# Starts of small tables and of the tiles behind them moved to multiples of 128 bytes, in a four-layer model on one core

## The chip, the cores and the metric

The program runs on one core of a Trainium2 chip. The metric is the device time of one execution in microseconds. Three runs of the kernel before gave 2496.11, 2497.12 and 2497.93 us; the median is 2497.12 us.

## What is computed

Two blocks of two layers each work on 256 tokens of width 1024 in float32. In the first block a layer is a mixer (projections of the normed input, a gated recurrence by chunks and three dilated attentions, two branches, an output projection) and a feed-forward with a squared ReLU. In the second block a layer is another mixer, then a dense SwiGLU (layer 0) or eight experts of which each token takes two (layer 1), then a gate. Cut to the large products:

```python
def first_block(...):
    for l in range(2):
        z = rms_norm(x, norm1_g[l]) @ w_in[l]                     # 1024 x 8704
        y = sigmoid(za) * (o_hg @ w_branch_a[l]) + sigmoid(zb) * (o_att @ w_branch_b[l])
        x = x + y @ w_out[l]
        x = x + square(relu(rms_norm(x, norm2_g[l]) @ w_up[l])) @ w_down[l]   # 4096 wide

def second_block(...):
    for i in range(2):
        h = h + hybrid_mixer(rmsnorm(h, norm_mix[i]), w_in[i], ..., w_out[i], i)
        xn = rmsnorm(h, norm_ffn[i])
        h = h + (swiglu(xn, ...) if i == 0 else moe_swiglu(xn, router, wg, wu, wd))
        h = h + sigmoid(rmsnorm(h, ple_norm[i]) @ ple_gate[i]) * (p[i] @ ple_proj[i])

def moe_swiglu(xn, router, wg, wu, wd):        # eight experts, 1024 x 3584 each, top two
    for e in range(8):
        out = out + combine[:, e:e+1] * ((silu(t @ wg[e]) * (t @ wu[e])) @ wd[e])
```

## The kernel before, in words

**The products.** Every weight matrix is cut into tiles of up to 512 rows by 512 columns, in the order of use (class `Plan`). `Kernel.ahead` fetches a tile by a DMA on SyncE's queue into a buffer `raw`, ScalarE rounds it to `hi` (line 435), VectorE takes the rest `lo = raw - hi` (line 436). An activation is turned by TensorE (`tr`, line 484) and split in the same way into a hi and a lo part (`tsplit`, lines 492 and 493; with a gain: `gained`, lines 501 and 503). `mm3` then makes each product of three matmuls, lines 450, 451 and 452: hi by hi, lo by hi, hi by lo. In each the activation's part, 128 by 128, is loaded into the array (here: the loaded operand), and the weight's part, 512 columns, streams past it. Each of the three loads its own 128 by 128, so every matmul has a load ahead of it.

**Where the loaded operands live.** `n` are the normed activations (pool `na`, whole program). `l` are split activations of the stage at hand (pool `lg`): in the first block they feed branches, output projection and down projection, in the second the projection of `p`, the output projection and the dense down projection, in the experts the down projections. The last expert's down operands are in a pool of their own, `lx`, named `x` in the profile. `o` is the 0/1 matrix that scatters an expert's rows back (lines 1508 and 1509). Operands of short matmuls are in `t`, `h` and others.

**What sets the addresses.** Tiles take addresses in the order in which their pools are opened, one behind the other, each rounded up to 32 bytes per partition. `const` and the weight buffers come first, then `sm` (small statistics, 64 bytes each, line 310), then `na`. For each stage `Kernel.open` lays a new scope behind that: `sc` (single tiles), `lg`, `tmp` and others. The second block first opens `ppp` and `sec` for good; `sec` holds the tables `tri`, `half` (2 columns, 8 bytes) and `iota`, which `fetch` (line 613) allocates, and the router's weights. In the experts, `route` (line 1389) first allocates `comb`, `rank`, `sel`, `count`, `most`, `rst`, then `unit` and the rows; the pools of the experts come behind them. Twelve bytes of `rst` or eight of `half` thus shift everything behind them in their scope.

**The order.** TensorE's order is the program's; the other engines are ordered by a scheduler. The change leaves the order of every engine as it was.

Of the kernel before, what the change touches and what calls it, by code (L numbers as in the profile page):

```python
# [10 lines left out]
BF16 = mybir.dt.bfloat16  # L11
U8 = mybir.dt.uint8
I32 = mybir.dt.int32
# [66 lines left out]
class Plan:  # L80


    def __init__(self):
        self.tiles = []
        self.specs = {}
        self.where = {}
        self.size = {}
        for l in range(2):
            self.first(l)
        self.mix2(0, lambda: self.rows("pp", 0))  # L90
        self.dense()
        self.gate2(0)
        self.mix2(1, lambda: self.rows("pp", 1))
        self.moe()
# [205 lines left out]
class Kernel:  # L300
    def __init__(self, tc, io, ctx):
        self.tc = tc
        self.nc = tc.nc
        self.io = io
        pool = lambda name, bufs, **k: ctx.enter_context(tc.tile_pool(name=name, bufs=bufs, **k))
        self.const = pool("const", 1)
        self.raw_p = pool("raw", RAW)
        self.hi_p = pool("hi", NSPLIT)
        self.lo_p = pool("lo", NSPLIT)
        self.sm = pool("sm", 40)  # L310
        self.na = pool("na", 8)
        self.acc_p = pool("acc", 4, space=PSUM)
        self.ms_p = pool("ms", 4, space=PSUM)
        self.scope = None
        self.plan = Plan()
        self.specs = self.plan.specs
        self.n_dma = self.n_split = self.n_used = 0
        self.rawt = {}
        self.split = {}
        self.flip = 0  # L320
        self.urgent = []
        self.tasks = []
        self.now = 0
        self.rate = 2
        self.grain = GRAIN1
        self.fetching = 0
        self.ring = deque([self.raw_p] * RAW)
        self.queue = None
# [284 lines left out]
    def fetch(self, name, dt=F32, pool=None):  # L613
        nc, src = self.nc, self.io["c_" + name]
        queue = self.queue or nc.gpsimd
        n = src.shape[1]
        t = (pool or self.sc).tile([128, n], dt, name=name)
        self.fetching += 1

        def gen():  # L620
            yield 3
            if dt == F32:
                queue.dma_start(t, src)
            else:
                for c in range(0, n, 384):
                    m = min(384, n - c)
                    r = self.T((128, m))
                    queue.dma_start(r, src[:, c:c + m])
                    nc.gpsimd.tensor_copy(t[:, c:c + m], r)
                    yield 1  # L630
            self.fetching -= 1
        self.push(gen())
        return t
# [755 lines left out]
    def route(self, norm, ms):  # L1389
        nc = self.nc  # L1390
        small = lambda name, shape, dt=F32: self.sc.tile([128, *shape], dt, name=name)
        self.comb, self.rank, self.sel = small("comb", (2, 8)), small("rank", (2, 8)), small("sel", (2, 8))
        self.count, self.most = small("count", (8,), I32), small("most", (1,), I32)
        self.rst = small("rst", (3, 2), BF16)
        self.unit = small("unit", (128,), BF16)
        nc.vector.tensor_copy(self.unit, self.ident)
        self.rows = [[[small(f"x{n}{b}{h}", (512,), BF16) for n in range(3)] for h in range(2)] for b in range(2)]
        self.need(lambda: ms[2] == 4)
        for h in range(2):
            for b in range(2):  # L1400
                self.thirds(self.xs(b, h), self.rows[b][h], self.T())
        self.spin(SPIN)
        with self.soon(HPR):
            top, s0, s1 = self.pick(ms[:2])

        def rest():
            yield 2
            cnt = self.M(8)
            for b in range(2):
                nc.tensor.matmul(cnt, self.ones, self.sel[:, b], start=b == 0, stop=b == 1)  # L1410
            self.thirds(norm.rst, [self.rst[:, n] for n in range(3)], self.S(2))
            e, g = self.S(2, 2), self.S(2, 2)
            R = norm.ready()
            for b in range(2):
                nc.vector.tensor_scalar(e[:, b, 0:1], top[:, b, 1:2], top[:, b, 0:1], R[b], op0=ALU.subtract, op1=ALU.mult)
            nc.scalar.activation(e[:, :, 1], e[:, :, 0], AF.Exp)
            nc.vector.tensor_scalar(e[:, :, 0], e[:, :, 1], 1.0, None, op0=ALU.add)
            nc.vector.reciprocal(g[:, :, 0], e[:, :, 0])
            nc.vector.tensor_mul(g[:, :, 1], g[:, :, 0], e[:, :, 1])
            for b in range(2):  # L1420
                nc.vector.tensor_scalar(s0[:, b], s0[:, b], g[:, b, 0:1], None, op0=ALU.mult)
                nc.vector.scalar_tensor_tensor(self.comb[:, b], s1[:, b], g[:, b, 1:2], s0[:, b], op0=ALU.mult, op1=ALU.add)
            most = self.S(1)
            nc.vector.tensor_reduce(most, cnt, axis=AX.X, op=ALU.max)
            nc.vector.tensor_copy(self.count, cnt)
            nc.vector.tensor_copy(self.most, most)
        self.push(rest())
# [398 lines left out]
```

## Time and profile before

| | us |
|---|---|
| median of three runs | 2497.12 |
| the profiled execution's own time | 2501.25 |
| its span, first to last instruction | 2499.4 |
| TensorE matmul busy | 2464.4 |
| VectorE busy | 1922.3 |
| ScalarE busy | 1618.6 |
| mean granted TensorE clock | 0.992 |

The profiled execution took 4.1 us longer than the median of the runs, and 1.9 us of its time lie outside the span. Busy times of TensorE are modelled: the record of one matmul reaches over the start of the next, so it is the distance from start to start, in the timeline, that says how fast matmuls follow one another. The first block runs from 0 to about 950 us, the second block without the experts to about 1470 us (its dense feed-forward from about 1100 to 1275 us), the experts from there to about 2460 us.

### The profile page before, as it was taken

How to read it: one execution, taken by the hardware profiler on the slowest of the kernel's cores; microseconds unless marked ns; L12 is line 12 of the kernel's file. 1: busy time of each engine (PE TensorE's matmuls, PEld its weight loads, DVE VectorE, ACT ScalarE, POOL GpSimd, SP SyncE). 2: the span in 40 equal slices, each digit the busy share in tenths (PEclk: the TensorE clock that was granted, in tenths of full speed). 3: DMA queues.
4: the chain of work that ended last, by engine and by line, in shares of the span. 5: the costliest groups of instructions: out<-in, count | busy, mean ns of one | idle time of the engine just before them, and what ended most of it. 6: DMA issues, size and time to landing. Idle time of an engine off the chain costs nothing. (4 is left out here: it accounts for less than half of the span.)

```text
span 2499.4 us, 33937 instructions
## 1 busy us (share of the span) xinstructions
PE 2464.4 (99%) x12113; PEld 2040.2 (82%) x12113; DVE 1922.3 (77%) x3330; ACT 1618.6 (65%) x2667; POOL 47.5 (2%) x66
## 2 busy tenths in 40 slices
PE   9999999999999999999999999999999999999998
PEld 7888888888888887888888878888888888888786
DVE  7775765578667656775576879999898989898888
ACT  7555555575556546654557567777777777777675
POOL 1000000100000002000001000000000000000000
PEclk9999999999999999999999989999999999999999
DMA  7443555553345555344564469999899999977895
GB/s 277 158 146 125 179 178 188 198 201 144 135 152 191 175 176 200 106 169 169 199 214 162 166 273 354 356 354 361 342 348 357 353 356 349 361 285 290 322 342 194
DMA packets 90530, 600.16 MB, mean 240 GB/s; under 512 B 12576, under 2 KB 14368, under 8 KB 19568
## 3 DMA queue, kind: packets, MB, share of 16 engines
q1 hardware_dynamic: 84240, 591.27, 64.2%
q10 hardware_dynamic: 4928, 3.16, 0.5%
q0 software_dynamic: 1184, 3.48, 0.4%
q8 instruction: 97, 1.59, 0.2%
q14 instruction: 81, 0.66, 0.1%
HBM read 596.82 MB, written 1.05 MB: 239 GB/s over the span
## 5 line engine op out<-in xcount | busy, mean ns | idle before, releaser
L436 DVE TENSOR_TENSOR lo<-raw,hi 128x512 fp32r<-128x512 f32 (+3 forms) x1584 | 1384.2, 911 | 315.9 <-ACT hi L435 296.7
L435 ACT CAST hi<-raw 128x512 fp32r<-128x512 f32 (+3 forms) x1584 | 1198.2, 800 | 422.6 <-PE a L451 340.1
L450 PE MATMUL a<-hi,n 128*128 128x512 f32 (+2 forms) x2176 | 867.9, 399 | 4.6 <-PEq L1661 3.5
L452 PE MATMUL a<-lo,n 128*128 128x512 f32 (+2 forms) x2176 | 848.9, 390 | 0.0
L451 PE MATMUL a<-hi,n 128*128 128x512 f32 (+2 forms) x2176 | 845.7, 389 | 1.7 <-DVE n L503 1.7
L452 PEld LDWEIGHTS a<-lo,n 128*128 128x128 f32 x2176 | 410.4, 189 | 93.3 <-DVE lo L436 5.1
L451 PEld LDWEIGHTS a<-hi,n 128*128 128x128 f32 x2176 | 411.7, 189 | 81.5 <-DVE n L503 3.2
L450 PEld LDWEIGHTS a<-hi,n 128*128 128x128 f32 x2176 | 411.1, 189 | 81.8 <-issue 4.2
L450 PE MATMUL a<-hi,l 128*128 128x512 f32 x552 | 220.3, 399 | 0.0
L452 PE MATMUL a<-lo,l 128*128 128x512 f32 x552 | 216.2, 392 | 0.0
L451 PE MATMUL a<-hi,l 128*128 128x512 f32 x552 | 216.1, 391 | 0.0
L492 ACT CAST l<-m 128x512 fp32r<-128x512 f32 (+1 forms) x126 | 70.2, 559 | 150.8 <-PE m L484 150.8
L450 PE MATMUL m<-hi,l 128*128 128x512 f32 x400 | 158.9, 397 | 0.7 <-ACT l L492 0.7
L451 PE MATMUL m<-hi,l 128*128 128x512 f32 x400 | 158.3, 396 | 0.2 <-DVE l L493 0.2
L452 PE MATMUL m<-lo,l 128*128 128x512 f32 x400 | 158.1, 395 | 0.0
L493 DVE TENSOR_TENSOR l<-m,l 128x512 fp32r<-128x512 f32 (+1 forms) x126 | 82.5, 658 | 62.4 <-ACT l L492 62.3
L452 PEld LDWEIGHTS a<-lo,l 128*128 128x128 f32 x552 | 103.7, 188 | 23.2
L451 PEld LDWEIGHTS a<-hi,l 128*128 128x128 f32 x552 | 103.8, 188 | 21.1
L450 PEld LDWEIGHTS a<-hi,l 128*128 128x128 f32 x552 | 103.7, 188 | 21.0
L484 PE MATMUL m<-ident,t 128*128 128x128 f32 x652 | 99.0, 272 | 2.8 <-DVE t L567 2.1
L484 PEld LDWEIGHTS m<-ident,t 128*128 128x128 f32 x652 | 80.3, 140 | 22.4 <-DVE t L567 2.6
L450 PEld LDWEIGHTS m<-hi,l 128*128 128x128 f32 x400 | 75.2, 188 | 18.4 <-ACT l L492 0.9
(302 smaller groups left out, 1784.7 us busy)
## 6 DMA issues: line engine op xcount, KB each, us to landing
raw<-in_w_dram SPq DMA_DIRECT2D x553, 1024.0 KB, 5.1
raw<-in_w_dram SPq DMA_DIRECT2D x10, 512.0 KB, 3.4
raw<-in_w_dram SPq DMA_DIRECT2D x4, 520.0 KB, 4.1
t<-in_c_dil_dram POOLq DMA_DIRECT2D x6, 192.0 KB, 2.9
x<-in_x_dram SPq DMA_DIRECT2D x4, 256.0 KB, 7.1
raw<-in_w_dram SPq DMA_DIRECT2D x4, 256.0 KB, 6.8
dec<-in_c_dec_dram POOLq DMA_DIRECT2D x2, 512.0 KB, 7.8
out_dram<-x SPq DMA_DIRECT2D x4, 256.0 KB, 2.0
```

What stands on the lines that cost most here:

```text
L435: nc.scalar.copy(hi[:, p], t[:, q])
L436: nc.vector.tensor_sub(lo[:, p], t[:, q], hi[:, p].bitcast(F32))
L450: mm(out, ah, wh, start=start, stop=False)
L451: mm(out, al, wh, start=False, stop=False)
L452: mm(out, ah, wl, start=False, stop=stop)
L484: self.nc.tensor.transpose(p[:, j], src[:, j * 128:(j + 1) * 128], self.ident)
L492: nc.scalar.copy(hi, p[:, :m])
L493: nc.vector.tensor_sub(lo, p[:, :m], hi.bitcast(F32))
```

## The change

The pool `sm` shrinks from 40 tiles to 38, that is by 128 bytes. `half` is allocated as 128 bytes, of which 8 are used. In `route`, `most` becomes 32 bytes, `rst` 32 bytes, and a tile `rest` of 96 bytes is allocated that nothing uses.

```diff
-        self.sm = pool("sm", 40)
+        self.sm = pool("sm", 38)
...
-        t = (pool or self.sc).tile([128, n], dt, name=name)
+        t = (pool or self.sc).tile([128, max(n, 32)], dt, name=name)[:, :n]
...
-        self.count, self.most = small("count", (8,), I32), small("most", (1,), I32)
-        self.rst = small("rst", (3, 2), BF16)
+        self.count, self.most = small("count", (8,), I32), small("most", (8,), I32)[:, 0:1]
+        self.rst = small("rst", (8, 2), BF16)[:, 0:3]
+        small("rest", (24,))
```

No instruction is added, removed or moved. What moves is the start of the tiles. In the built programs the loaded operands of matmuls with 512 streamed columns start at these places, in bytes past a multiple of 256 (the 128 loaded columns are 512 bytes wide, so all slices of a tile share its place):

```
loaded operand, and where               matmuls   before   after
n, all projections from a norm             6336        0     128
l, first block                             1152        0     128
l, second block before the experts          504       32       0
l, experts                                 1200       64     128
x, last expert                              144       64     128
o, scatter                                   64       64     128
streamed hi and lo, everywhere                -        0       0
```

In the second block and the experts the tiles `t`, the rows (bfloat16) and the tables move in the same way, from 32 or 64 bytes past a multiple of 128 to a multiple of 128. The `raw` buffers at the far end of the memory stay where they were.

With 38 tiles in the ring of `sm` a tile comes round two allocations sooner, so one wait for GpSimd stands earlier. On VectorE, in the attention of the second block's mixer (line 1086 finds a row's maximum, lines 1221 and 1222 mix two softmaxes; `Pool_49` is GpSimd's semaphore), as a piece of the difference:

```order
 L1221 TENSOR_SCALAR t<-t,s 128x256
 L1088 TENSOR_SCALAR s<-s 128x1 [waits DVE_49]
-L1086 ISA t,s<-m,caus 128x256 [waits PE_49]
+L1086 ISA t,s<-m,caus 128x256 [waits PE_49,Pool_49]
 L1086 ISA s 128x1
 L1222 SCALAR_TENSOR_TENSOR t<-t,s 128x256 [waits DVE_49]
 L1088 TENSOR_SCALAR s<-s 128x1 [waits DVE_49]
-L1086 ISA t,s<-m,caus 128x128 [waits PE_49,Pool_49]
+L1086 ISA t,s<-m,caus 128x128 [waits PE_49]
```

The wait moved four rows up, from one maximum to the one before it; the same happens once in the second mixer, and once on ScalarE.

## Rows read from the trace of the kernel before

**Rows 1.** The page, part 1: busy us (share of the span) and instructions.
```profile
span 2499.4 us, 33937 instructions
PE 2464.4 (99%) x12113; PEld 2040.2 (82%) x12113; DVE 1922.3 (77%) x3330; ACT 1618.6 (65%) x2667; POOL 47.5 (2%) x66
```
**Rows 2.** Windows: us, busy PE, PEld, DVE, ACT, POOL, clock, DMA share, GB/s.
```profile
1200.00:1300.00 100.00, 100.00 (x498) 83.51 (x497) 63.10 (x136) 55.20 (x123) 2.06 (x4) 1.00 0.58 203
...
1500.00:1600.00 100.00, 100.00 (x487) 81.74 (x486) 93.14 (x92) 79.96 (x89) 0.00 (x0) 1.00 0.94 359
```
**Rows 3.** Waits, SyncE 1500:2000, ScalarE and TensorE 2000:2400: us in total, times, longest.
```profile
SPq L418 <- DVE lo L436: 420.9, 164, 6.1
...
ACT hi L435 <- DMA raw<-in_w_dram: 1.0, 2, 0.6
...
PE a L450 <- PEq L1661: 3.5, 1, 3.5
```
**Rows 4.** Timeline of PE, first block, down projection, operand at 0: start us, busy us.
```profile
456.00 0.39 PE L450 MATMUL a<-hi,l 128*128 128x512 f32 x1
...
458.72 0.39 PE L450 MATMUL a<-hi,l 128*128 128x512 f32 x1
```
**Rows 5.** Timeline of PE, first block, branch projection, operand at a multiple of 256.
```profile
261.34 0.39 PE L452 MATMUL a<-lo,l 128*128 128x512 f32 x1
...
263.15 0.39 PE L451 MATMUL a<-hi,l 128*128 128x512 f32 x1
```
**Rows 6.** Timeline of PE, second block, dense down projection, operand at 32.
```profile
1250.43 0.40 PE L450 MATMUL a<-hi,l 128*128 128x512 f32 x1
...
1253.23 0.40 PE L450 MATMUL a<-hi,l 128*128 128x512 f32 x1
```
**Rows 7.** Timeline of PE, experts: down projection (l at 64), then up (n at 0).
```profile
1610.26 0.39 PE L452 MATMUL m<-lo,l 128*128 128x512 f32 x1
...
1613.06 0.39 PE L452 MATMUL m<-lo,l 128*128 128x512 f32 x1
...
1616.08 0.39 PE L450 MATMUL a<-hi,n 128*128 128x512 f32 x1
...
1617.67 0.39 PE L451 MATMUL a<-hi,n 128*128 128x512 f32 x1
```
**Rows 8.** Timeline of PE, first block, just behind short matmuls, operand at 0.
```profile
150.92 0.39 PE L451 MATMUL a<-hi,n 128*128 128x512 f32 x1
...
153.00 0.39 PE L451 MATMUL a<-hi,n 128*128 128x512 f32 x1
```
**Rows 9.** Groups by form, line 452, a third of each product's matmuls.
```profile
L452 PE MATMUL a<-lo,n 128*128 128x512 f32 x2112 | 830.8, 393 | 0.0
...
L452 PE MATMUL a<-lo,l 128*128 128x512 f32 x552 | 216.2, 392 | 0.0
...
L452 PE MATMUL m<-lo,l 128*128 128x512 f32 x400 | 158.1, 395 | 0.0
...
L452 PE MATMUL m<-lo,x 128*128 128x512 f32 x48 | 19.2, 399 | 0.3 <-DVE lo L436 0.3
```
**Rows 10.** Line 492, first block, then experts: duration ns min/median/max, first and last start.
```profile
L492 ACT CAST l<-m x48: 573/578/587, 128.9 to 859.5; 128x512 fp32r<-128x512 f32 x48
...
L492 ACT CAST l<-m x47: 573/585/587, 1512.1 to 2326.0; 128x512 fp32r<-128x512 f32 x47
```
**Rows 11.** Timelines of POOL and DVE, mixer of the second block's layer 1.
```profile
1328.27 0.60 POOL L1247 TENSOR_SCALAR l<-tri,s 128x128 f32<-128x128 f32 x1
...
1337.95 0.28 DVE L1086 CUSTOM_DVE_ANT_0 t<-m,caus 128x128 f32<-128x128 f32 x1
```
**Rows 12.** Timeline of PE, dense up projection, 256 columns, operand at 0.
```profile
1203.61 0.28 PE L452 MATMUL a<-lo,n 128*128 128x256 f32 x1
...
1205.04 0.28 PE L452 MATMUL a<-lo,n 128*128 128x256 f32 x1
```

## The prediction

> **What bounds the kernel now.** I began with the busy times: TensorE is busy for 99% of the span, VectorE for 77% [rows 1]. A modelled busy time proves little, so the windows came next. In the dense down projection and all through the experts TensorE shows no idle time; in the experts VectorE is at 93 of 100 us and the DMAs at 0.94 of theirs, at 359 GB/s [rows 2]. Then the waits say who follows whom. From 2000 to 2400 us TensorE's longest wait is 3.5 us at the branch of the overflow path, ScalarE waits 1.0 us in all for weights to land, and SyncE's queue waits 420.9 us of 500 for VectorE to give a buffer back [rows 3]. So weights are ready early and fetches are held up by buffers: TensorE sets the pace, and a nanosecond taken off each of its matmuls should come off the end, so long as nothing else is that close.
>
> The decisive view is the timeline of TensorE, read from start to start. In long runs of equal matmuls, 512 columns each, the reader is to divide the distance of two starts by the matmuls between them:
>
> - loaded operand at a multiple of 512 bytes: 12 matmuls from 456.00 to 458.72, 226.7 ns each [rows 4];
> - at a multiple of 256: 8 from 261.34 to 263.15, 226.3 ns [rows 5];
> - 32 bytes past a multiple of 128, dense down projection: 12 from 1250.43 to 1253.23, 233.3 ns [rows 6];
> - 64 bytes past it, experts' down projection: 12 from 1610.26 to 1613.06, 233.3 ns; three microseconds later, in the same stage, the up projection with n at 0: 7 from 1616.08 to 1617.67, 227.1 ns [rows 7].
>
> [...] The streamed operand is at 0 everywhere, so it explains nothing.
>
> **The change part by part.**
>
> *Loaded operands at 32 or 64 bytes.* The groups give a third of the matmuls each [rows 9]: m<-lo,l 400 and m<-lo,x 48 are the experts' down projections, 3 x 448 = 1344 matmuls; of a<-lo,l's 552 the placement puts 384 at 0 and 168 at 32, so 3 x 168 = 504 matmuls of the second block. If the load then costs what it costs in rows 4, each gains 6.7 ns. That isn't quite so where short matmuls stand ahead: there nine matmuls with an operand at 0 take 2.08 us, 231.1 ns [rows 8], and the gain would be 2.2 ns. Bounds for the 1848: 12.3 us if all are in long runs, 4.1 us if none is. The experts' downs come in runs of 24 that follow other long matmuls, as around rows 7, so I take the full 6.7 ns: 9.0 us. In the second block's projections about a quarter stand behind transposes or attention (117 of 453 recorded, counted along the timeline): 504 x (0.75 x 6.7 + 0.25 x 2.2) = 2.8 us. Sum **11.8 us**.
>
> *Small ones.* The 64 scatter loads of `o` (0 to 0.4 us), and the first three matmuls behind each experts' down run, which take 0.69 us where 0.68 would do (1615.39 to 1616.08 by the same timeline; some 50 times, 0.5 us). The gathers' bfloat16 operands move too; no row has them at a multiple of 128, and I take 0, with 0 to 1 us for the range. Transposes of `t` at 32 and 64 show the same 272 ns as those at 0: nothing.
>
> *VectorE, ScalarE, DMAs.* Their tiles move as well. ScalarE's line 492 writes l at 0 in the first block and at 64 in the experts: medians 578 and 585 ns, minimum 573 in both [rows 10]. Nothing to gain there, and nothing on the path. The `raw` buffers don't move.
>
> *The ring of 38.* The earlier wait for GpSimd stands on VectorE's line 1086. GpSimd is done at 1328.87, the first such instruction starts at 1337.95 [rows 11]; in the mixer before and on ScalarE the distance is no smaller. It costs nothing; without those 9 us of lead, VectorE and the split of weights behind it would wait for GpSimd.
>
> *What goes the other way.* To free bytes, `sm` lost 128, and n and the first block's l moved from 0 to 128 past a multiple of 256. No row of this trace shows a matmul of 512 columns with its operand there. Cost 0 if 128 is as good as 256, and 6.7 ns for each of 7488 matmuls if it isn't (a rival below). [...]
>
> [...]
>
> The profiled execution would go from 2501.25 to 2489.5 us. It stands 4.1 us above the median of the runs, so the median goes from 2497.12 to 2485.3; I say **2485 us**.
>
> **The rivals.**
>
> *Blocks of 256 bytes (slower).* [...] It decides at n, whose start goes to 128 past 256. Price: (6336 + 1152) x 6.7 = 50 us more, less 504 x 6.7 = 3 us for the second block's l, which goes to 0; the experts' downs stay as slow as they are. That is 2497 + 47 = 2544 at most; with a third of the n matmuls behind short ones, where the loss is 2.2 ns, 2533. I take 2538.
>
> *The start is not the cause (no change).* The chains at 233 ns are all of later stages, so stage and start go together; then the time stays at 2497. Against it: within the experts, 3 us apart, n runs at 227 and l at 233 [rows 7], and the dense down projection has the form of the first block's [rows 4, 6].
>
> [...]
>
> *The DMAs become the bound of the experts.* TensorE would ask for 0.9% more than 359 GB/s at a share of 0.94 [rows 2]. For it: that is close. Against it: 1.0 us of waiting for weights [rows 3]. Then the 9.0 us are lost and 2.8 stay: 2494.3.
>
> **How the numbers follow.** A difference of 0.2%, 5 us, is about what a measurement of this kernel can tell from none. Forecast 0.78 (14.2 us, 2482.9, with long runs throughout and all small gains; 2493 at the lower bound of 4.1 us), slower by blocks of 256 0.12, no change 0.05, DMAs 0.05. Range 2482 (2482.9 less the 0.9 us by which runs scatter) to 2494.5: the forecast and the DMA case, 0.83. Faster 0.78; same 0.10, which is no change and the DMA case; slower 0.12.
>
> **What would show it.** Right: the runs that answer to rows 6 and 7 fall to 2.72 us for 12 matmuls, those of rows 4, 5 and 12 stay, the experts' stage ends some 12 us earlier. Wrong: n at 233 ns in the first block, so that the down projection of rows 4 comes microseconds late; or downs still at 233; or downs at 227 while TensorE waits for `lo` or ScalarE for `raw` in the experts.

## The result, and the profile after

The changed kernel takes 2522.39 us (median of 5 runs, 2518.39 to 2523.40) against 2497.12 us for the kernel before beside it (2495.80 to 2501.16): a ratio of 1.0091, 95% interval 1.0079 to 1.0102. (The ratios are those on record for all runs of a comparison, not quotients of two medians; that quotient is 1.0101 here.) It is slower by 25.3 us where 12 us less was forecast, and 28 us above the upper end of the range.

The profiled execution took 2522.39 us, its span is 2520.6 us. Its page, part 1 (busy us, share of the span, instructions), answers to [rows 1]:

```profile
PE 2486.7 (99%) x12113; PEld 2043.2 (81%) x12113; DVE 1922.6 (76%) x3330; ACT 1619.5 (64%) x2667; POOL 46.9 (2%) x66
```

The instructions are the same in number. TensorE's busy time grew by 22.3 us and the span by 21.2; VectorE and ScalarE are where they were, within 1 us. The window, columns as in [rows 2], shows no idle time of TensorE either, and its longest wait from 2000 to 2420 us is still the one at the branch of the overflow path, 3.9 us where [rows 3] have 3.5:

```profile
1500.00:1600.00 100.00, 100.00 (x483) 81.22 (x482) 92.03 (x91) 78.86 (x88) 0.00 (x0) 1.00 0.95 361
```

So TensorE still sets the pace, at the same granted clock of 1.00 in this stretch, and its matmuls follow one another more slowly. The timeline of TensorE says which. First block, down projection, l now 128 past a multiple of 256 (before: [rows 4]):

```profile
455.91 0.39 PE L450 MATMUL a<-hi,l 128*128 128x512 f32 x1
...
458.69 0.40 PE L450 MATMUL a<-hi,l 128*128 128x512 f32 x1
```

Twelve matmuls in 2.78 us, 231.7 ns each, where it was 226.7. Second block, l now at a multiple of 256 (before at 32: [rows 6]):

```profile
1265.13 0.39 PE L451 MATMUL a<-hi,l 128*128 128x512 f32 x1
...
1267.85 0.39 PE L451 MATMUL a<-hi,l 128*128 128x512 f32 x1
```

Twelve in 2.72 us, 226.7 ns instead of 233.3: the gain that was forecast for it. Experts, down projection (l from 64 to 128), then up (n from 0 to 128), as in [rows 7]:

```profile
1625.46 0.39 PE L450 MATMUL m<-hi,l 128*128 128x512 f32 x1
...
1628.25 0.40 PE L450 MATMUL m<-hi,l 128*128 128x512 f32 x1
...
1631.04 0.39 PE L450 MATMUL a<-hi,n 128*128 128x512 f32 x1
...
1633.13 0.40 PE L450 MATMUL a<-hi,n 128*128 128x512 f32 x1
```

The down projection stays slow, 2.79 us for twelve (232.5 ns, before 233.3); n now takes 232.2 ns, 9 in 2.09 us, where it took 227.1. Two of the stretches in the rows of before don't lose. Just behind short matmuls, as in [rows 8], nine matmuls still take 2.08 us; and with 256 columns, as in [rows 12], twelve still take 1.43 us:

```profile
152.26 0.39 PE L451 MATMUL a<-hi,n 128*128 128x512 f32 x1
...
154.34 0.39 PE L451 MATMUL a<-hi,n 128*128 128x512 f32 x1
...
1218.15 0.28 PE L451 MATMUL a<-hi,n 128*128 128x256 f32 x1
...
1219.58 0.28 PE L451 MATMUL a<-hi,n 128*128 128x256 f32 x1
```

To turn such stretches into a sum, all distances from start to start of 512-column matmuls that follow one another, up to 260 ns, were averaged along the timeline for each product, and the difference to before was multiplied by the product's number of matmuls:

```
                            before    after    matmuls    difference
n                           228.67   232.62      6336      +25.0 us
l, first block              227.45   232.49      1152       +5.8
l, second block             233.27   227.59       504       -2.9
l and x, experts            233.28   232.56      1344       -1.0
sum                                                        +26.9      (measured +25.3)
```

The means of l in the experts stand for x as well. n's mean before is above 226.7 because of the stretches behind short matmuls. The whole loss is thus in place: n and the first block's l pay 30.8 us, and the two gains are worth 3.9.

### The profile page after: what moved, and what is told of

The parts are those of the page before. It is cut to its first block, busy times and chain, and to the rows that moved or that the text cites. A ratio compares the mean times of both kernels' runs of the same rounds, so it can differ in the third digit from the quotient of the medians.

```text
span 2520.6 us, 33937 instructions
## 1 busy us (share of the span) xinstructions
PE 2486.7 (99%) x12113; PEld 2043.2 (81%) x12113; DVE 1922.6 (76%) x3330; ACT 1619.5 (64%) x2667; POOL 46.9 (2%) x66
```

## The experiments

Three theories could explain this. **Blocks of 256**: a loaded operand is slow wherever its own start isn't a multiple of 256. **Ring**: the shorter ring of `sm` holds VectorE up, and the starts only go with it. **Padding**: the larger tiles cost the time. The first comparison tests these; its kernel before took 2498.60 us (median).

**All wide tiles at multiples of 256.** A ring of 32, `half` of 256 bytes, and a longer `rest`:

```diff
-        self.sm = pool("sm", 38)
+        self.sm = pool("sm", 32)
...
-        t = (pool or self.sc).tile([128, max(n, 32)], dt, name=name)[:, :n]
+        t = (pool or self.sc).tile([128, max(n, 64)], dt, name=name)[:, :n]
...
-        small("rest", (24,))
+        small("rest", (56,))
```

> Ring of 32 sm buffers; half, the last tile of the small-table area and the route tables padded so that n and every wide tile start at a multiple of 256 bytes (in the experts 256 past a multiple of 512). Theory 'blocks of 256' (a loaded operand of 128 float32 columns is slow wherever its start is not a multiple of 256): n and the first block's l stay at 227 to 229 ns, the second block's l goes from 233.3 to 227.6 (504 x 5.7 = 2.9 us), the experts' down projections from 233.4 to 227.6 (1344 x 5.8 = 7.8 us): 2497.1 - 10.7 = 2486.4 us. Theory 'ring' (the shorter ring of sm makes VectorE wait for GpSimd, the starts are only a sign of it): a ring of 32 is shorter still than 38, so at least 2522 us. Theory 'padding' (the larger tiles of the second block or the experts cost the time): about 2522 us.

Measured: 2490.27 us, ratio 0.9959, interval 0.9945 to 0.9972. Its experts' down projection:

```profile
1606.50 0.39 PE L450 MATMUL m<-hi,l 128*128 128x512 f32 x1
...
1609.22 0.39 PE L450 MATMUL m<-hi,l 128*128 128x512 f32 x1
```

226.7 ns each. On its page TensorE's busy time is 2452.4 us, 12.0 less than in [rows 1], and the ring of 32 and the larger padding cost nothing that can be seen. Ring and padding fall.

**The change with a ring of 36.** Everything behind `sm` lies 128 bytes lower, the padding is the change's:

```diff
-        self.sm = pool("sm", 38)
+        self.sm = pool("sm", 36)
```

> The change with a ring of 36 instead of 38 sm buffers, so that everything behind it lies 128 bytes lower: n and the first block's l at multiples of 256 again, the experts' wide tiles at a multiple of 256 too, the second block's l 128 past one. Blocks of 256: n and first l as before, second l from 233.3 to 232.5 (504 x 0.8 = 0.4 us), experts' downs 1344 x 5.8 = 7.8 us: 2497.1 - 8.2 = 2488.9 us. Ring: 2522 us or more. Padding: about 2522 us, since the padding is that of the change.

Measured: 2490.59 us, ratio 0.9969 (0.9958 to 0.9980). The mean of n is 228.5 ns again, of the experts' l 226.8, of the second block's l 232.3. One number in the first line of the change decides between a gain and a loss.

**n alone moved.** In the kernel before:

```diff
-        self.sm = pool("sm", 40)
-        self.na = pool("na", 8)
+        self.sm = pool("sm", 36); pool("gap", 1).tile([128, 32], F32, name="gap")
+        self.na = pool("na", 8); pool("gap2", 1).tile([128, 32], F32, name="gap2")
```

> The kernel before with n alone moved: 4 sm buffers fewer, 128 unused bytes ahead of n's pool and 128 behind it, so that only n lies 128 past a multiple of 256 and all else where it was. Blocks of 256: 6336 matmuls with n from a mean of 228.7 to 232.6 ns, 24.9 us: 2522.0 us; l's intervals as before. If n's start costs nothing and the loss of the change lies in l or elsewhere: 2497 us.

Measured: 2520.81 us, ratio 1.0083 (1.0068 to 1.0099). The mean of n is 232.75 ns, all three l's are within 0.2 ns of before. n's start alone carries most of the loss.

**The streamed operands alone moved.** A control, and the test of a fourth theory, which the expectation calls relation. In the kernel before, a ring of 38 and 128 bytes ahead of the weight buffers, so that hi and lo start at 128 (and `raw` 128 bytes higher), and all else stays.

```diff
-        self.raw_p = pool("raw", RAW)
+        pool("gap", 1).tile([128, 32], F32, name="gap"); self.raw_p = pool("raw", RAW)
...
-        self.sm = pool("sm", 40)
+        self.sm = pool("sm", 38)
```

> The kernel before with a ring of 38 sm buffers and 128 unused bytes ahead of the raw, hi and lo pools: the streamed operands hi and lo lie 128 past a multiple of 256, n, l and everything behind them exactly where they were. Blocks of 256 by the loaded operand's own start: 2497.1 us, n at 228.7. Theory 'relation' (what counts is the distance of the loaded operand's start from the streamed one's, which the change made 128 for n): n and first l slow, 24.9 + 5.8 us: 2527.8 us. Ring: 2522 us, since the ring is the change's 38.

Measured: 2523.18 us, ratio 1.0093 (1.0078 to 1.0109): slow, with every loaded operand exactly where the fast kernel had it. First block's l at 0, then the experts' l at 64, in its timeline:

```profile
455.08 0.39 PE L450 MATMUL a<-hi,l 128*128 128x512 f32 x1
...
457.88 0.39 PE L450 MATMUL a<-hi,l 128*128 128x512 f32 x1
...
1611.25 0.39 PE L450 MATMUL m<-hi,l 128*128 128x512 f32 x1
...
1613.99 0.39 PE L450 MATMUL m<-hi,l 128*128 128x512 f32 x1
```

l at 0 goes from 226.7 to 233.3 ns, and l at 64, slow before, to 228.3 in this stretch (2.74 us for twelve). Blocks of 256 by the loaded operand's own start falls, and so does a theory in which each operand needs a good start of its own, since the experts' l got faster by making the other operand's start worse. What is left is **relation**: the distance from the streamed operand's start to the loaded one's, modulo 256. I still set it against that last theory, **both starts**, in the next comparison (kernel before: 2499.14 us).

**The change, with the streamed operands moved along.** Every loaded operand stays where the change puts it:

```diff
-        self.raw_p = pool("raw", RAW)
+        pool("gap", 1).tile([128, 32], F32, name="gap"); self.raw_p = pool("raw", RAW)
...
-        self.sm = pool("sm", 38)
+        self.sm = pool("sm", 36)
```

> The change with every start as the change has it (n, first block's l and the experts' l 128 past a multiple of 256, second block's l at one), and only the streamed operands moved: 2 sm buffers fewer and 128 unused bytes ahead of raw, hi and lo, so that hi and lo too lie 128 past a multiple of 256. Theory 'relation' (a matmul is fast when the loaded operand's start lies a multiple of 256 from the streamed one's, whatever either is): n, first l and experts' l fast again, the second block's l at a distance of 128 and slow: 2497.1 - 1344 x 5.8 ns - 504 x 0.8 ns = 2488.9 us. Theory 'both starts' (each operand has to start at a multiple of 256 by itself): the loaded starts are the change's and the streamed ones now off too: 2522 us or more.

Measured: 2487.88 us, ratio 0.9960 (0.9946 to 0.9974). Experts, down and then up, all of them with both operands 128 past a multiple of 256:

```profile
1603.15 0.39 PE L450 MATMUL m<-hi,l 128*128 128x512 f32 x1
...
1605.87 0.39 PE L450 MATMUL m<-hi,l 128*128 128x512 f32 x1
...
1608.59 0.39 PE L450 MATMUL a<-hi,n 128*128 128x512 f32 x1
...
1610.63 0.39 PE L450 MATMUL a<-hi,n 128*128 128x512 f32 x1
```

226.7 ns for both. The same starts that made the changed kernel slow are fast here.

**Everything moved together.** The same gap in the kernel before, with the ring left at 40:

> The kernel before with 128 unused bytes ahead of raw, hi and lo and the ring left at 40: everything behind them lies 128 bytes higher, loaded and streamed operands alike, with every distance between them as before. Relation: 2497.1 us, n at 228.7, the experts' l at 233.4. Both starts: all of n and the first block's l slow, 24.9 + 5.8 us: 2527.8 us.

Measured: 2498.43 us, ratio 0.9995 (0.9985 to 1.0005): no change, as relation has it. n's mean is 228.4 ns with both operands at 128, the experts' l stays at 233.3.

**The first line of the change alone**, a ring of 38 and no padding:

> The first line of the change alone, without the padding: n and the first block's l 128 past a multiple of 256, the second block's l 160 and the experts' 192 past one, streamed operands at 0. Relation: n and first l cost 24.9 + 5.8 us; the experts' l at a distance of 192, which the run with the streamed operands moved showed at 229.3 ns, gain 1344 x 4.1 ns = 5.5 us; the second block's l at 160 between 229.3 and 233.3, 0 to 2 us: 2497.1 + 30.7 - 5.5 = 2522.3, down to 2520.3 us. Both starts: 192 is as slow as 64 was: 2527.8 us.

Measured: 2521.51 us, ratio 1.0089 (1.0072 to 1.0106); expected by relation 2522.3. The experts' l, at a distance of 192, is at a mean of 230.1 ns, the second block's, at 160, at 233.5.

**The streamed operands at 64**, a ring of 39 and a gap of 64 bytes:

> The kernel before with a ring of 39 and 64 unused bytes ahead of raw, hi and lo: streamed operands 64 past a multiple of 256, all else where it was. Relation: the experts' l (64 past) now at a distance of 0 and fast, 1344 x 5.8 = 7.8 us less; n and the first block's l at a distance of 192, 229.3 ns by the run with 128, or up to 1.5 ns more for n behind short matmuls: n 3.8 to 13.3 us more, first l 2.4 us more; together 2495.5 to 2505 us, and up to 2 us less if the second block's l at 224 gains. Both starts: n and the first block's l slow, the experts' l no better: 2527.8 us.

Measured: 2497.45 us, ratio 0.9993 (0.9983 to 1.0003), inside relation's 2495.5 to 2505. The experts' l, now at a distance of 0, falls from 233.3 to 227.2 ns, n at 192 rises by 0.7 ns, the first block's l by 1.4. Matmuls with 256 columns got faster, at a distance of 192:

```profile
1204.82 0.28 PE L452 MATMUL a<-lo,n 128*128 128x256 f32 x1
...
1205.84 0.28 PE L452 MATMUL a<-lo,n 128*128 128x256 f32 x1
```

Nine in 1.02 us are 113.3 ns, where [rows 12] have 119.2.

**Only lo moved**, a ring of 38 and the gap of 128 bytes between `hi` and `lo` (kernel before beside it: 2499.74 us):

> The kernel before with a ring of 38 and 128 unused bytes between the pools hi and lo: only the streamed operand lo, a third of the matmuls (line 452), lies 128 past a multiple of 256. Theory 'relation, matmul by matmul': line 452 alone pays: n 2112 x 3.9 ns = 8.2 us, the first block's l 384 x 5 = 1.9 us, and the experts' l on lo gains 448 x 4.1 = 1.8 us: 2497.1 + 8.3 = 2505.4 us. Theory 'neighbours' (a matmul off its distance slows the one ahead or behind as well, so that two of three pay): 2497.1 + 16.6 = 2513.7 us.

Measured: 2518.61 us, ratio 1.0074 (1.0057 to 1.0091). Both expectations missed, from the same side: with a third of the matmuls off, about three quarters of the loss comes that the run with all streamed operands off has (18.9 of 24.6 us). Experts, up projection:

```profile
1627.54 0.39 PE L450 MATMUL a<-hi,n 128*128 128x512 f32 x1
1627.77 0.40 PE L451 MATMUL a<-hi,n 128*128 128x512 f32 x1
1628.00 0.40 PE L452 MATMUL a<-lo,n 128*128 128x512 f32 x1
1628.24 0.39 PE L450 MATMUL a<-hi,n 128*128 128x512 f32 x1
```

All three lines are slow: from line 450 to 451 the mean for n is 231.8 ns, from 451 to 452 232.0, from 452 to 450 231.1, against 229.1, 228.1 and 229.0 before. What one matmul loses is not its own affair: the two distances that begin with a matmul on hi, at a distance of 0, grow by 2.7 and 3.9 ns, the one that begins with a matmul on lo by 2.1. The experts' down projection, where hi stays at a distance of 64 and lo goes to 192, looks local all the same: from line 452 to 450 the mean falls from 233.5 to 228.7 ns, the other two by about 1 ns or less.

**A distance of 96**, 96 unused bytes ahead of `sm` (kernel before: 2498.32 us):

> The kernel before with 96 unused bytes ahead of sm: streamed operands at 0, n and the first block's l at a distance of 96, the second block's l at 128, the experts' l at 160. It fills the one gap in the distances tried (0, 32, 64, 128, 160, 192 and 224). If 96 lies with its neighbours 64 and 128 (233.4 and 232.5 ns): n 6336 x 3.9 to 4.5 ns = 25 to 28.5 us, first l 1152 x 5 to 5.9 ns = 5.8 to 6.8 us, second l 0.4 us less: 2498 + 30 to 35 = 2528 to 2533 us. If some distance other than 0 suits 512 columns better, as 192 suits 256 columns (113.3 instead of 119.2 ns in the run with the streamed operands at 64): 2498 us or less.

Measured: 2535.54 us, ratio 1.0150 (1.0133 to 1.0167), slower than its neighbours gave. n's mean is 234.1 ns. No distance better than 0 was found for 512 columns.

The sum by products, made as for the changed kernel, beside what was measured (median less that of the kernel before in the same comparison), in us:

```
                               n    l first   l second   experts     sum   measured
change                      +25.0     +5.8      -2.9      -1.0     +26.9     +25.3
all at 256                   -0.9      0.0      -3.0      -8.7     -12.6      -8.3
change, ring of 36           -1.0      0.0      -0.5      -8.7     -10.2      -8.0
n alone                     +25.9      0.0      -0.1      -0.3     +25.5     +22.2
streamed at 128             +25.5     +6.7      +0.1      -5.1     +27.2     +24.6
change, streamed at 128      -2.6     -0.2      -0.3      -8.7     -11.8     -11.3
all moved by 128             -1.5     -0.2      -0.1       0.0      -1.8      -0.7
ring of 38 alone            +24.4     +5.8      +0.1      -4.2     +26.1     +22.4
streamed at 64               +4.7     +1.6       0.0      -8.2      -1.9      -1.7
lo alone at 128             +18.9     +4.3      -0.4      -2.3     +20.5     +18.9
distance 96                 +34.2     +7.7      -0.4      +0.2     +41.7     +37.2
```

The sums have the sign of every run and come near its size; they are up to 4.5 us off. Most of that comes from giving every matmul the mean of the pairs: multiplied by the pairs alone (5788 for n, 1094, 468, and 1322 in the experts), they come within 1.4 us of what was measured, but for all at 256, where they are 3.0 us off. The means hang a little on which pairs are taken: from the unrounded starts the first block's l is at 227.8 ns before, and a product's sum moves by up to 0.6 us.

## Why the prediction was wrong

- **What bounds the kernel: right.** TensorE set the pace in each of these runs. In all of them its distances from start to start give the change of the time to within 4.5 us.
- **Loaded operands at 32 or 64 bytes: right for the second block, wrong for the experts.** 2.8 us were forecast for the second block's l and 2.9 came, in part by luck: its new start at 0 helps because the streamed operands start there too, which the forecast didn't ask for (at 128, with the streamed operands at 128 as well, n was as fast: 228.4 ns, before 228.7). The experts were to give 9.0 and gave 1.0, because 128 is nearly as slow as 64 with the streamed operand at 0 (232.6 against 233.3 ns); at a distance of 0 they do give 8.7 (all at 256).
- **What goes the other way: the step that failed.** Of the two prices that the prediction names for n and the first block's l at 128, 0 and 6.7 ns a matmul, its sum holds 0. That 0 was my estimate: no row showed such a matmul, as the prediction itself says, and no run shows one at 128 as fast as one at a multiple of 256 while the streamed operands are at 0 (231.7 ns in the first block, where it was 226.7). The term measured +25.0 us for n and +5.8 for the first block's l, against which the gains, 3.9 us, are small.
- **"The streamed operand is at 0 everywhere, so it explains nothing": the deeper mistake.** An operand that never moves in a trace can't be excluded by it. With hi and lo at 0, a start and a distance are the same number; the run that moved hi and lo alone parted them.
- **"If the load then costs what it costs in rows 4, each gains 6.7 ns": not so simply.** 6.7 ns is what twelve matmuls of [rows 6] or [rows 7] take more than those of [rows 4], per matmul; no run shows it to be a price of the load alone. Such a price would show at both widths, but with n at 128 the 256-column matmuls lose nothing (119.2 ns, as in [rows 12]), and at a distance of 192 they gain 6 ns (113.3) while the 512-column ones lose 0.7 (n) to 1.4 (first block's l).
- **The rival "blocks of 256 bytes": right in sign and place, wrong in reason and price.** It had n decide, and n did. But starts at 128 are fast when the streamed operand is there too (226.7 ns, the change with the streamed operands moved along), and 6.7 ns a matmul, 50 us, measured 3.9 ns for n and 5.0 for the first block's l, 30.8 us: a long run loses about 5, and in the stretch just behind short matmuls nothing is seen to be lost, where 2.2 had been allowed. (By its own terms the lower end of that rival is 2534 us, not 2533.)
- **The rival "start is not the cause"** fell with the same runs. "DMAs become the bound" was put to the test by the kernel with all at 256: its matmuls run at 226.7 ns, and its window, columns as in [rows 2], has TensorE busy throughout with the DMAs at 363 GB/s and a share of 0.94:

```profile
1500.00:1600.00 100.00, 100.00 (x492) 82.60 (x491) 93.65 (x95) 80.91 (x92) 0.00 (x0) 1.00 0.94 363
```

- **The small costs at nothing** (the ring, VectorE, ScalarE): right; a ring of 32 costs nothing either.

## What to carry to other kernels

When matmuls with their own load each follow one another without a gap, compare the start of the loaded operand with that of the streamed one, modulo 256 bytes: at a distance of 0 this kernel's 512-column matmuls took 226.7 ns in long runs, elsewhere mostly 232 to 234 (229 to 230 at 192). Here it took no absolute alignment, only that the two pools agreed: both at 128 were as fast as both at 0 (n's mean 228.4 against 228.7 ns). Starts were tried at multiples of 32 bytes alone, with float32 operands of 128 loaded columns. A change in the number of small buffers ahead of a pool can move the distance unseen: here two buffers fewer in `sm` cost 22.4 us in the kernel before, and two fewer again won 31.8 in the changed one. Before a trace is used to exclude a cause, ask whether that cause varies in it at all.

## What had not been expected of the hardware

- The distance of the two operands' starts, modulo 256, sets the rate, as the table has it. Means of start-to-start for l with 512 columns, by product, from before, the change and the experiments in which all streamed operands start alike:

```
distance, bytes (loaded start less streamed start)      ns
  0                                                     226.8 to 227.6
 32                                                     233.3
 64                                                     233.3
 96                                                     234.2
128                                                     232.3 to 233.3
160                                                     233.4 to 233.5
192                                                     228.9 to 230.1
224                                                     233.3
```

- It repeats after 256 bytes and not after 128: loaded operands at a multiple of 512 and at an odd multiple of 256 are alike, 226.7 and 226.3 ns ([rows 4], [rows 5]), and 128 differs from 0 (232.3 to 233.3 against 226.8 to 227.6 ns).
- It isn't symmetric: 64 costs 6.5 ns (226.8 to 233.3 in the experts) and 192 between 1.4 (first block) and 3.3 (experts).
- It isn't local: with lo alone off, the n matmuls that stream hi slow down as well, by 2.7 and 3.9 ns.
- It depends on the width: for 256 columns 192 is better than 0 (113.3 against 119.2 ns).

What in the chip makes the distance count, and why one streamed operand in three is enough to disturb the rest, stays open: no run here shows it.
